# Sample tokens of two heads in one score product, and no products with 32 weight columns

## Chip, cores, metric

One core of a Trainium2 chip runs the whole kernel. The metric is the device time of one execution in microseconds, the median of the runs shown. Its engines are TensorE (PE, with weight loads as PEld), VectorE (DVE), ScalarE (ACT), GpSimd (POOL) and SyncE (SP, which issues most DMAs).

## What is computed

One layer of a streaming encoder for 1,024 prompt tokens and 32 sample tokens. Two branches of it matter here. Branch A is attention with 16 heads of width 64 over 2 key and value heads; a sample token reads 128 cached keys and the 32 new ones:

```python
kblk = jnp.concatenate([k_prev.astype(ka.dtype), ka], axis=1)[:, None]
vblk = jnp.concatenate([v_prev.astype(va.dtype), va], axis=1)[:, None]
...
s = jnp.einsum('bnqkgd,bnskd->bnkgqs', q, k).astype(jnp.float32) * (A_HEAD_DIM ** -0.5)
s = s + bias.astype(jnp.float32)[None, None]
...
m = jnp.maximum(jnp.max(s, axis=-1, keepdims=True), sink)
p = jnp.exp(s - m)
denom = jnp.sum(p, axis=-1, keepdims=True) + jnp.exp(sink - m)
return jnp.einsum('bnkgqs,bnskd->bnqkgd', (p / denom).astype(v.dtype), v)
```

Branch B is a gated linear recurrence with 8 heads and a state of 128 × 128, evaluated in blocks; the 32 sample tokens are a block of their own with a state that is given:

```python
o = jnp.einsum('bhld,bhdv->bhlv', q_ * jnp.exp(b_), state)
a = jnp.einsum('bhtd,bhsd->bhts', q_ * jnp.exp(b_ - b_mid), k_ * jnp.exp(b_mid - b_))
o = o + jnp.einsum('bhts,bhsv->bhtv', jnp.where(causal, a, 0.0), v_)
state = (jnp.exp(b_last)[:, :, 0, :, None] * state
         + jnp.einsum('bhsd,bhsv->bhdv', k_ * jnp.exp(b_last - b_), v_))
```

The outputs of both are gated, projected and added, and a feed-forward part follows. It takes more than half of the time and the change doesn't touch it.

## The kernel before

Tokens stand in three groups, `GR`: 384, 384 and 288 columns; group 2 holds 256 prompt tokens and the 32 sample tokens (from column `SO` = 256). `token_tiles` cuts the groups into nine tiles of 128 tokens, the last of which has the 32 sample tokens. Large products run in float32r, as three products of a high and a low part. Transposes are products of float32 with the identity as the moving operand, so that what is transposed is the weight operand, and a tile of 32 tokens is one of 32 weight columns. The products inside the recurrence are plain float32, and the profile shows each as two passes.

*Attention.* `stream` runs over blocks of gate and query projections, and hands out small steps between half blocks ("half-steps"). Eight pairs of heads `i` follow each other; pair `i`'s nine tiles `j` are spread over the half-steps `lo_` to `hi_` of one pair: `scores(i, j)` at some half-step, `turn(i, j)` three later, `values` five later. Pair 7 has six half-steps for its nine tiles. `q_out` writes the queries of a pair, one head per buffer (`qa`, `qb`), each as high and low part over 128 partitions; for group 2 the columns behind the 288 are zeroed on GpSimd. `scores` makes, per head, two products (parts of the keys, `K1` and `K2`), adds the bias and takes the extremum in one DVE instruction (L457), copies the sink on GpSimd (L455), takes the exponential on ACT (L462), and scales (L464, L466). For the sample (`j` = 8) each product has 160 columns and 32 used rows, one head beside the other in the free dimension of `sc8`, the one buffer that all pairs share. `turn` transposes the probabilities (L478), four times for the sample, and splits them into high and low parts (`ph`, `pl`); `values` multiplies them with `Vs`. `bias_load` loads a pair's bias from DRAM on SP's queue into one of two buffers (L429) and sets two corners on GpSimd.

*Recurrence.* Pieces of the projections of head h (`qf_unit`, then `io_unit`, 11 pieces each) run on PE, and small steps of head h stand behind them at piece numbers counted from `m0` (the head's first piece) and `m1` = `m0` + 22. `factors` makes the decayed keys `ke`, queries `tq` and `qx`, and `d1`. `k_turn` transposes the keys of a group into `kk` (L1186), `v_turn` the values into `vk` (L1115). `tile_in` makes the state's update (L1207) and the products of keys and queries (L1211 for the sample, L1215 for the others), `tile_out` the outputs (L1247 and L1249), `group_out` transposes back (L1270). For the sample, L1211, L1247 and L1249 use 32 weight columns.

The order of each engine is the order of the text as far as the framework's scheduler keeps it; it sets the waits between engines itself. SP and GpSimd work off their queues in order.

Of the kernel before, what the change touches and what calls it, by code (L numbers as in the profile page):

```python
# [10 lines left out]
F32 = mybir.dt.float32  # L11
# [48 lines left out]
def layer_kernel(  # L60
# [17 lines left out]
    def nm(s):  # L78
        n_names[0] += 1
        return f"{s}_{n_names[0]}"  # L80
# [231 lines left out]
    with right("ap") as ap:  # L312
# [89 lines left out]
        def q_out(i):  # L402
            def out(g, b):
                n = GR[g][1]
                qa = ap.tile([P, 384], F32R, tag="qa", name=nm("qa"), bufs=4)
                qb = ap.tile([P, 384], F32R, tag="qb", name=nm("qb"), bufs=4)
                if g == 2:
                    G.memset(qa[:, n:384].bitcast(F32), 0.0)
                    G.memset(qb[:, n:384].bitcast(F32), 0.0)
                S.mul(qa[0:64, :n], b[0:64, :n], -0.125)  # L410
                V.scalar_tensor_tensor(qa[64:128, :n], b[0:64, :n], -0.125, qa[0:64, :n].bitcast(F32),
                                       op0=ALU.mult, op1=ALU.subtract)
                S.mul(qb[64:128, :n], b[64:128, :n], -0.125)
                V.scalar_tensor_tensor(qb[0:64, :n], b[64:128, :n], -0.125,
                                       qb[64:128, :n].bitcast(F32), op0=ALU.mult, op1=ALU.subtract)
                qs[i, g] = (qa, qb)
            return out
# [3 lines left out]
        def bias_load(i):  # L421

            bias = aq.tile([P, 2, 256], F32, tag="bias", name=nm("bias"), bufs=2)
            for h in range(2):

                row = rb_d[2 * i + h]
                src = bass.AP(tensor=row.tensor, offset=row.offset + 127,
                              ap=[[368, 8], [383, 16], [1, 256]])
                dma(bias[:, h, :], src)  # L429
            G.memset(bias[0:64, :, 192:256], BIG)  # L430
            G.memset(bias[64:128, :, 0:64], BIG)
            biases[i] = bias
            yas[i] = aq.tile([P, T], F32, tag="ya", name=nm("ya"), bufs=2)

        def span(j):
# [5 lines left out]
            return P, (j - 1) * P, 256, 0, ((j - 1, 0, P), (j, P, P))  # L441

        def scores(i, j):
            m_, k0, nk, b0, tl = span(j)
            e_ = b0 + nk
# [3 lines left out]
            for h, q in enumerate(qs[i, g]):  # L449
                o = s[:, h * 256 + b0:h * 256 + e_]  # L450
                E.matmul(o, q[:, c:c + P], K1[kv][:, k0:k0 + nk], start=True, stop=False)
                E.matmul(o, q[:, c:c + P], K2[kv][:, k0:k0 + nk], start=False, stop=True)
            sc = sc8 if j == 8 else aq.tile([P, 2, 260], F32, tag="sc", name=nm("sc"), bufs=5)
            st = aq.tile([P, 2, 2], F32, tag="st", name=nm("st"), bufs=4)
# [15 lines left out]
        def turn(i, j):  # L470
            m_, k0, nk, b0, tl = span(j)
            sc = probs[i, j]
# [3 lines left out]
            for a, (_, kc, _) in enumerate(tl):  # L476
                for h in range(2):
                    E.transpose(t[:, (2 * a + h) * P:(2 * a + h + 1) * P], sc[:, h, kc:kc + P],  # L478
                                ident[:])
            n = 2 * len(tl)  # L480
            ph, pl = (x[:].rearrange("p a b -> p (a b)")[:, :n * m_] for x in (ph, pl))
            if m_ == P:
                split(ph, pl, t[:, :n * P])
            else:
                split(*(x.rearrange("p (a b) -> p a b", b=m_) for x in (ph, pl)),
                      t[:].rearrange("p (a b) -> p a b", b=P)[:, :, :m_])
            probs[i, j] = (ph, pl)
# [361 lines left out]
        bias_load(0)  # L849
        sc8 = aq.tile([P, 2, 2 * P], F32, name="sc8")  # L850
        G.memset(sc8[:], 0.0)
        for b, out in zip(banks[1], outs):
            out(1, b)
        blocks, small = [(lambda w=w: w, 2, out) for w, out in zip(ws, outs)], {}
        for i in range(8):
# [131 lines left out]
    with right("bp") as bp:  # L987
# [120 lines left out]
        def v_turn(h, g):  # L1108
# [4 lines left out]
            t = tr_bank()  # L1113
            for i, (c, m_, smp) in enumerate(token_tiles(g)):
                E.transpose(t[:m_, i * P:(i + 1) * P], vt[:, c:c + m_], ident[:])  # L1115
            S.copy(vk[:, 0:f, :], t[:, :f * P].rearrange("p (a b) -> p a b", b=P))
            if g == 2:
                S.copy(vk_s[:32], t[:32, 2 * P:3 * P])

# [9 lines left out]
        def factors(h, g):  # L1129
# [50 lines left out]
        def k_turn(h, g):  # L1180
# [3 lines left out]
            kk = bp.tile([P, 3, P], F32, tag="kk", name=nm("kk"), bufs=2)  # L1184
            for i, (c, m_, smp) in enumerate(token_tiles(g)):
                E.transpose(t[:m_, i * P:(i + 1) * P], ke[:, c:c + m_], ident[:])  # L1186
            f = 3 if g < 2 else 2
            S.copy(kk[:, 0:f, :], t[:, :f * P].rearrange("p (a b) -> p a b", b=P))
            if g == 2:
                S.copy(kk[:32, 2, :], t[:32, 2 * P:3 * P])  # L1190
                G.memset(kk[32:64, 2, :], 0.0)
                G.memset(kk[64:P, 2, :], 0.0)
            d["kk", g] = kk

        def tile_in(h, j):
# [14 lines left out]
            if smp:  # L1210
                E.matmul(s[:32, 0:32], d1[:, c:c + 32], qx[:, 384:416], start=True, stop=True)  # L1211
                V.tensor_tensor(ai[:32, :32], s[:32, 0:32].bitcast(I32), cmask[:32, :32],
# [23 lines left out]
        def tile_out(h, j):  # L1236
# [9 lines left out]
            vk = vk_s if smp else d["vk", g][:, i, :]  # L1246
            E.matmul(b[:m_, 0:P], am[:, :m_], vk[:], start=True, stop=st is None)  # L1247
            if st is not None:
                E.matmul(b[:m_, 0:P], d["tq", g][:, c:c + m_], st[:], start=False, stop=True)  # L1249
            S.copy(vk[:m_], b[:m_, 0:P])  # L1250
# [36 lines left out]
        for h in range(8):  # L1287
# [871 lines left out]
```

## Time and profile before

| | |
|---|---|
| median of 3 runs | 1993.48 us (1993.47 to 1995.96) |
| profiled execution | 1993.55 us |
| its span, first to last instruction | 1991.8 us |
| PE busy | 1974.8 us |
| granted TensorE clock | 0.999 |

A row of the profile names the line, engine and operation, output and inputs by the program's names, the shapes and the count. For a product, `128*32 128x160` means 128 rows and 32 columns of weights, and a moving operand of 128 × 160. Behind the bar stand busy time, the mean of one in ns, and the engine's idle time ahead of them with what ended it. In the timeline, a row has its start, its duration (of all, where several are merged), and in brackets the idle time ahead of it. Matmuls overlap, since each is counted from its start to its modelled end; what one costs is the distance to the next start.

### The profile page before, as it was taken

The numbers are of one execution on the slowest core, as the hardware profiler recorded it, in microseconds if no ns is written. First come the engines' busy times: TensorE is split into PE (matmuls) and PEld (weight loads), VectorE is DVE, ScalarE is ACT, GpSimd is POOL, SyncE is SP. The second block draws the span as 40 slices with busy tenths as digits, with TensorE's granted clock in tenths as the row PEclk, the third lists the DMA queues.
The fourth block names the chain that finished last, engine by engine and source line by source line (L and its number), as shares of the span: only waits on it lengthen the run. The fifth ranks groups of instructions, "written<-read, shape, count | busy, mean of one in ns | idle before, by whom it ended". The sixth has DMA issues, their size and how long they took to land.

```text
span 1991.8 us, 37378 instructions
## 1 busy us (share of the span) xinstructions
PE 1974.8 (99%) x14303; PEld 1954.3 (98%) x14303; DVE 1422.5 (71%) x3130; ACT 962.7 (48%) x2151; POOL 235.4 (12%) x345
## 2 busy tenths in 40 slices
PE   8999999999999999999999999999999999999998
PEld 8999999999999999999999999999999999999998
DVE  6788888688888888553455778787888884655552
ACT  7555566566666666451225663333333344444332
POOL 1211100000000000002001123333333300000000
PEclk9999999999999999999999999999999999999999
DMA  7622311411111111486558572222222245665542
GB/s 256 169 88 89 98 55 63 142 43 58 58 49 46 46 46 54 140 246 208 170 177 281 183 266 85 66 88 74 76 86 76 86 152 192 214 194 168 167 133 78
DMA packets 253640, 247.48 MB, mean 124 GB/s; under 512 B 13893, under 2 KB 221912, under 8 KB 253461
## 3 DMA queue, kind: packets, MB, share of 16 engines
q1 hardware_dynamic: 245141, 218.59, 35.6%
q0 software_dynamic: 8240, 26.44, 3.7%
q8 instruction: 112, 1.84, 0.4%
q14 instruction: 67, 0.55, 0.1%
q10 hardware_dynamic: 80, 0.07, 0.0%
HBM read 177.56 MB, written 65.32 MB: 122 GB/s over the span
## 4 chain that ended last, share of the span: by engine, by line
PE 91%; DVE 4%; ACT 1%; issue 1%; DMA 1%; POOL 0%; SPq 0%; DVEq 0%; POOLq 0%; ACTq 0%
PE mm L200 14%; PE mm L201 14%; PE mm L202 14%; PE st L1882 7%; PE st L1881 7%; PE st L1880 7%; PE Y L1018 2%; PE G L1021 2%; PE G L1020 2%; PE G L1018 2%; PE Y L1021 2%; PE Y L1020 2%; PE tr L478 1%; PE so L1215 1%; PE Z L1021 1%
## 5 line engine op out<-in xcount | busy, mean ns | idle before, releaser
L1880 PE MATMUL st<-op,wt 128*128 128x264 f32 x1232 | 348.6, 283 | 1.9 <-DVE Sp L1893 1.2
L1882 PE MATMUL st<-op,wt 128*128 128x264 f32 x1232 | 349.8, 284 | 0.0
L1881 PE MATMUL st<-op,wt 128*128 128x264 f32 x1232 | 347.6, 282 | 0.0
L184 DVE TENSOR_TENSOR wl<-wr,wh 128x1024 fp32r<-128x1024 f32 x129 | 157.9, 1224 | 121.4 <-ACT wh L181 111.0
L1880 PEld LDWEIGHTS st<-op,wt 128*128 128x128 f32 x1232 | 231.2, 188 | 3.5 <-DVE Sp L1893 1.7
L1881 PEld LDWEIGHTS st<-op,wt 128*128 128x128 f32 x1232 | 231.4, 188 | 0.0
L1882 PEld LDWEIGHTS st<-op,wt 128*128 128x128 f32 x1232 | 230.8, 187 | 0.0
L181 ACT CAST wh<-wr 128x1024 fp32r<-128x1024 f32 x116 | 121.7, 1050 | 198.0 <-PE mm L201 124.8
L200 PE MATMUL mm<-La,wh 128*128 128x384 f32 (+1 forms) x528 | 174.4, 331 | 0.0
L201 PE MATMUL mm<-Lb,wh 128*128 128x384 f32 (+1 forms) x528 | 170.9, 324 | 0.5 <-DVE Lb L717 0.5
L200 PE MATMUL mm<-ac,wh 128*128 128x352 f32 x528 | 170.6, 323 | 0.0
L202 PE MATMUL mm<-La,wl 128*128 128x384 f32 (+1 forms) x528 | 170.4, 323 | 0.2 <-DVE wl L692 0.2
L202 PE MATMUL mm<-ac,wl 128*128 128x352 f32 x528 | 169.6, 321 | 0.0
L201 PE MATMUL mm<-ac,wh 128*128 128x352 f32 x528 | 169.3, 321 | 0.0
L1640 ACT CAST wt<-wu 128x512 fp32r<-128x512 f32 x126 | 77.9, 619 | 186.6 <-POOL ab L1866 88.3
L200 PE MATMUL mm<-Ra,wh 128*128 128x264 f32 x512 | 145.4, 284 | 0.0
L201 PE MATMUL mm<-Rb,wh 128*128 128x264 f32 x512 | 145.0, 283 | 0.0
L202 PE MATMUL mm<-Ra,wl 128*128 128x264 f32 x512 | 145.0, 283 | 0.0
L1641 DVE TENSOR_TENSOR wt<-wu,wt 128x512 fp32r<-128x512 f32 x126 | 103.0, 820 | 38.8 <-ACT wt L1640 38.8
L462 ACT ACTIVATE sc<-sc,st 128x257 f32<-128x257 f32 (+1 forms) x144 | 69.7, 485 | 79.2 <-DVE st L457 79.0
L201 PEld LDWEIGHTS mm<-Lb,wh 128*128 128x128 f32 x528 | 99.4, 188 | 1.6 <-DVE Lb L717 1.4
L202 PEld LDWEIGHTS mm<-La,wl 128*128 128x128 f32 x528 | 99.3, 188 | 0.5 <-DVE wl L692 0.5
(511 smaller groups left out, 5701.5 us busy)
## 6 DMA issues: line engine op xcount, KB each, us to landing
wr<-in_w_down_dram SPq DMA_DIRECT2D x66, 512.0 KB
wu<-in_w_up_dram SPq DMA_DIRECT2D x42, 512.0 KB
wu<-in_w_in_dram SPq DMA_DIRECT2D x32, 512.0 KB
wr<-in_w_in_dram SPq DMA_DIRECT2D x25, 512.0 KB
ac<-act_d SPq DMA_DIRECT2D x66, 176.0 KB
act_d<-Up SPq DMA_DIRECT2D x21, 528.0 KB
wr<-in_w_out_dram SPq DMA_DIRECT2D x16, 512.0 KB
pw_d<-pw POOLq DMA_DIRECT2D x11, 512.0 KB, 5.7
```

What stands on the lines that cost most here:

```text
L181: S.copy(hi[:], raw[:])
L184: V.tensor_tensor(lo[:], raw[:], hi[:].bitcast(F32), op=ALU.subtract)
L200: E.matmul(ps, wh, a, start=first and n == 0, stop=False)
L201: E.matmul(ps, wh, b, start=False, stop=False)
L202: E.matmul(ps, wl, a, start=False, stop=last and n == len(ks) - 1)
L1018: E.matmul(o, wh, x[0][k], start=first and k == 0, stop=False, skip_group_check=True)
L1020: E.matmul(o, wh, x[1][k], start=False, stop=False, skip_group_check=True)
L1021: E.matmul(o, wl, x[0][k], start=False, stop=k == 3, skip_group_check=True)
L1641: V.tensor_tensor(t[:, 1], src, t[:, 0].bitcast(F32), op=ALU.subtract)
L1880: E.matmul(o, wh, xh, start=first and k == 0, stop=False, skip_group_check=True)
L1881: E.matmul(o, wh, xl, start=False, stop=False, skip_group_check=True)
L1882: E.matmul(o, wl, xh, start=False, stop=k == 3, skip_group_check=True)
```

## The change

In attention, the sample tokens of both heads of a pair become one tile of 64 rows. Their queries stand side by side in `qa`, the second head's copied there on GpSimd; one product each for `K1` and `K2` gives both heads' scores; a bias tile of its own (`bias8`, one buffer, loaded on SP in the same way) and sinks of both heads in `nsink8` make one addition, one exponential and one scaling; two transposes follow. In the recurrence, the sample's values are copied on GpSimd into the key tile behind its keys and transposed with them, in `k_turn`, which now comes after `v_turn`; L1211, L1247 and L1249 take 128 weight columns, the added ones zero. The buffers change in size to fit.

```diff
                 if g == 2:
-                    G.memset(qa[:, n:384].bitcast(F32), 0.0)
-                    G.memset(qb[:, n:384].bitcast(F32), 0.0)
+                    G.memset(qa[:, n + 32:384].bitcast(F32), 0.0)
...
+                if g == 2:
+                    G.tensor_copy(qa[:, n:n + 32], qb[:, SO:n].bitcast(F32))
...
+        def bias_load8(i):
+            bias8 = aq.tile([64, 160], F32, tag="bias8", name=nm("bias8"), bufs=1)
+            for h in range(2):
+                row = rb_d[2 * i + h]
+                src = bass.AP(tensor=row.tensor, offset=row.offset + 127,
+                              ap=[[368, 2], [383, 16], [1, 160]])
+                dma(bias8[32 * h:32 * h + 32, :], src)
+            biases[i, 8] = bias8
             yas[i] = aq.tile([P, T], F32, tag="ya", name=nm("ya"), bufs=2)
...
+        def scores8(i):
+            s, q, kv, m_ = s_bank(), qs[i, 2][0], i // 4, 64
+            E.matmul(s[:, 0:160], q[:, SO:SO + P], K1[kv][:, 1024:1184], start=True, stop=False)
+            E.matmul(s[:, 0:160], q[:, SO:SO + P], K2[kv][:, 1024:1184], start=False, stop=True)
+            st = aq.tile([P, 2, 2], F32, tag="st", name=nm("st"), bufs=4)
+            mx, tot = st[:m_, 0, 0:1], st[:m_, 1, 0:1]
+            G.tensor_copy(sc8[:m_, 160:161], nsink8[:m_, i:i + 1])
+            V.tensor_tensor_reduce(out=sc8[:m_, 0:160], in0=s[:m_, 0:160], in1=biases[i, 8][:],
+                                   scale=1.0, scalar=nsink8[:m_, i:i + 1], op0=ALU.add,
+                                   op1=ALU.min, accum_out=mx)
+            S.activation(sc8[:m_, 0:161], sc8[:m_, 0:161], AF.Exp, bias=mx, scale=-1.0,
+                         accum_out=tot)
+            V.reciprocal(tot, tot)
+            V.tensor_scalar(sc8[:m_, 0:160], sc8[:m_, 0:160], tot, None, op0=ALU.mult)
...
+            if j == 8:
+                for a in range(2):
+                    E.transpose(t[:, a * P:(a + 1) * P], sc8[:, a * P:(a + 1) * P], ident[:])
+                split(*(x.rearrange("p (a b) -> p a b", b=64) for x in (ph, pl)),
+                      t[:, 0:2 * P].rearrange("p (a b) -> p a b", b=P)[:, :, :64])
...
+            small.setdefault(lo_ + (4 if i < 7 else 0), []).insert(0, lambda i=i: bias_load8(i))
             if i < 7:
                 small.setdefault(lo_ + 2, []).insert(0, lambda i=i: bias_load(i + 1))
...
-        vk_s, am_s = (bp.tile([P, n], F32, name=nm("z")) for n in (P, 32))
+        vk_s, am_s = (bp.tile([P, P], F32, name=nm("z")) for _ in range(2))
...
             for i, (c, m_, smp) in enumerate(token_tiles(g)):
+                if smp:
+                    d["vt_s"] = vt[:, c:c + m_]
+                    break
                 E.transpose(t[:m_, i * P:(i + 1) * P], vt[:, c:c + m_], ident[:])
...
-            qx = bt("qx", 576, 3)
+            qx = bt(*(("qx", 576, 2) if g < 2 else ("qx2", 416, 1)))
...
+            if g == 2:
+                for t in (d1, d["tq", g]):
+                    G.memset(t[:, n:GMAX], 0.0)
...
+                if smp:
+                    G.tensor_copy(ke[:, c + m_:c + 2 * m_], d.pop("vt_s"))
+                    m_ *= 2
                 E.transpose(t[:m_, i * P:(i + 1) * P], ke[:, c:c + m_], ident[:])
...
                 S.copy(kk[:32, 2, :], t[:32, 2 * P:3 * P])
+                S.copy(vk_s[:32], t[32:64, 2 * P:3 * P])
...
-                E.matmul(s[:32, 0:32], d1[:, c:c + 32], qx[:, 384:416], start=True, stop=True)
+                E.matmul(s[:, 0:32], d1[:, c:c + P], qx[:, 384:416], start=True, stop=True)
...
-            E.matmul(b[:m_, 0:P], am[:, :m_], vk[:], start=True, stop=st is None)
+            E.matmul(b[:, 0:P], am[:], vk[:], start=True, stop=st is None)
             if st is not None:
-                E.matmul(b[:m_, 0:P], d["tq", g][:, c:c + m_], st[:], start=False, stop=True)
+                E.matmul(b[:, 0:P], d["tq", g][:, c:c + P], st[:], start=False, stop=True)
...
-            at(m1 + 6, k_turn, h, 2)
-            at(m1 + 8, v_turn, h, 2)
+            at(m1 + 7, v_turn, h, 2)
+            at(m1 + 8, k_turn, h, 2)
```

More of the change, by code (lines that the diff above doesn't have):

```diff
@@ L441, in span @@
             return P, (j - 1) * P, 256, 0, ((j - 1, 0, P), (j, P, P))
+        def scores8(i):
[12 more added lines that the diff above has]
+            V.tensor_scalar(sc8[:m_, 0:160], sc8[:m_, 0:160], tot, None, op0=ALU.mult)
         def scores(i, j):
+            if j == 8:
+                scores8(i)
+                return
             m_, k0, nk, b0, tl = span(j)
@@ L452, in scores @@
                 E.matmul(o, q[:, c:c + P], K2[kv][:, k0:k0 + nk], start=False, stop=True)
-            sc = sc8 if j == 8 else aq.tile([P, 2, 260], F32, tag="sc", name=nm("sc"), bufs=5)
+            sc = aq.tile([P, 2, 260], F32, tag="sc", name=nm("sc"), bufs=5)
             st = aq.tile([P, 2, 2], F32, tag="st", name=nm("st"), bufs=4)
@@ L471, in turn @@
             m_, k0, nk, b0, tl = span(j)
-            sc = probs[i, j]
+            sc = probs.get((i, j))
             ph = aq.tile([P, 2, 2 * P], F32R, tag="ph", name=nm("ph"), bufs=4)
@@ L475, in turn @@
             t = tr_bank()
[L476 to L483, printed above, removed]
-            else:
-                split(*(x.rearrange("p (a b) -> p a b", b=m_) for x in (ph, pl)),
-                      t[:].rearrange("p (a b) -> p a b", b=P)[:, :, :m_])
+            n = 2 * len(tl) * m_
+            ph, pl = (x[:].rearrange("p a b -> p (a b)")[:, :n] for x in (ph, pl))
+            if j == 8:
+                for a in range(2):
+                    E.transpose(t[:, a * P:(a + 1) * P], sc8[:, a * P:(a + 1) * P], ident[:])
+                split(*(x.rearrange("p (a b) -> p a b", b=64) for x in (ph, pl)),
+                      t[:, 0:2 * P].rearrange("p (a b) -> p a b", b=P)[:, :, :64])
+            else:
+                for a, (_, kc, _) in enumerate(tl):
+                    for h in range(2):
+                        E.transpose(t[:, (2 * a + h) * P:(2 * a + h + 1) * P], sc[:, h, kc:kc + P],
+                                    ident[:])
+                split(ph, pl, t[:, :n])
             probs[i, j] = (ph, pl)
@@ L849, in layer_kernel @@
         bias_load(0)
-        sc8 = aq.tile([P, 2, 2 * P], F32, name="sc8")
+        sc8 = aq.tile([P, 2 * P], F32, name="sc8")
         G.memset(sc8[:], 0.0)
+        nsink8 = aq.tile([64, 8], F32, name="nsink8")
+        for h in range(2):
+            z = slice(32 * h, 32 * h + 32)
+            G.tensor_copy(nsink8[z], nsink[z].rearrange("p (i h) -> p i h", h=2)[:, :, h])
         for b, out in zip(banks[1], outs):
@@ L1114, in v_turn @@
             for i, (c, m_, smp) in enumerate(token_tiles(g)):
+                if smp:
+                    d["vt_s"] = vt[:, c:c + m_]
+                    break
                 E.transpose(t[:m_, i * P:(i + 1) * P], vt[:, c:c + m_], ident[:])
             S.copy(vk[:, 0:f, :], t[:, :f * P].rearrange("p (a b) -> p a b", b=P))
-            if g == 2:
-                S.copy(vk_s[:32], t[:32, 2 * P:3 * P])
         def decay(h):
```

## The prediction

> **What bounds the kernel.** I read the first parts of the page, then busy time by stretch, then the timeline of TensorE around the sample instructions.
>
> ```profile
> PE 1974.8 (99%) x14303; PEld 1954.3 (98%) x14303; DVE 1422.5 (71%) x3130; ACT 962.7 (48%) x2151; POOL 235.4 (12%) x345
> ...
> PE 91%; DVE 4%; ACT 1%; issue 1%; DMA 1%; POOL 0%; SPq 0%; DVEq 0%; POOLq 0%; ACTq 0%
> ```
>
> TensorE (PE) is busy for 99% of the span and carries 91% of the chain that ended last. Busy time of overlapping matmuls says little by itself, so the next view matters more: the two stages that the diff touches, cut into stretches. Columns are the stretch, its length, then busy time of PE, PEld, DVE, ACT and POOL, the granted clock, the DMA share and GB/s.
>
> ```profile
> 92.00:345.00 253.00, 253.00 (x1774) 251.81 (x1774) 210.89 (x656) 144.95 (x442) 26.20 (x103) 1.00 0.24 78
> 345.00:370.00 25.00, 23.98 (x172) 23.28 (x171) 15.94 (x53) 13.36 (x40) 0.93 (x6) 1.00 0.15 53
> ...
> 412.00:842.00 430.00, 428.49 (x2851) 420.12 (x2852) 353.98 (x1003) 267.80 (x721) 3.19 (x16) 1.00 0.20 60
> ```
>
> Through nearly all of attention (92 to 345 us) PE has no idle time at all: 253.00 of 253.00, at full clock. Only pair 7, whose nine score tiles are squeezed into half a unit's steps, has a hole of 1.0 us (345 to 370). In the recurrence (412 to 842) 1.5 us are missing out of 430. So a PE slot saved in these stages should come off the end almost whole, as long as no other engine becomes late. DVE at 211 of 253 us is the nearest to that.
>
> **The change, part by part.** Busy times of PE overlap, so I cost by the distance between starts.
>
> *Scores of the sample tokens.* Before, four products of 160 columns (two heads, K1 and K2) per pair; after, two. Transposes before four, after two.
>
> ```profile
> 140.26 0.24 PE L451 MATMUL s<-K,qa 128*128 128x160 f32 x1
> ...
> 140.67 0.34 PE L200 MATMUL mm<-La,wh 128*128 128x288 f32 x1
> ...
> 446.36 0.49 PE L1115 MATMUL tr<-ident,vt 128*128 128x128 f32 x3
> 446.69 0.39 PE L1247 MATMUL so<-vk,am 128*128 128x128 f32 x2
> ```
>
> The four products (two of L451, two of L452) last from 140.26 to 140.67, 0.41 us; two fewer save half of it, 0.20. Three transposes of the same size in the recurrence last 0.33 us, 0.11 each; two fewer save 0.22. Per pair 0.42 us, over eight pairs 3.4 us.
>
> *The sample product of the recurrence.* Per head, six passes (each f32 product runs as two) have 32 weight columns.
>
> ```profile
> 462.26 0.33 PE L1021 MATMUL X<-La,wt 128*128 128x384 f32 x1
> 462.43 0.38 PE L1247 MATMUL so<-vk,am 128*128 128x128 f32 x2
> 462.65 0.39 PE L1249 MATMUL so<-S,tq 128*128 128x128 f32 x2
> 462.87 0.39 PE L1207 MATMUL so<-z,kk 128*128 128x128 f32 x2
> 463.19 0.25 PE L1211 MATMUL so<-qx,d 128*32 128x32 f32 x2
> 463.37 0.55 PE L1186 MATMUL tr<-ident,ke 128*128 128x128 f32 x3
> ...
> 467.26 0.34 PE L1021 MATMUL Y<-TH,wt 128*128 128x384 f32 x1
> 467.53 0.41 PE L1247 MATMUL so<-z,z 128*32 128x128 f32 x2
> 467.78 0.38 PE L1249 MATMUL so<-S,tq 128*32 128x128 f32 x2
> 468.09 0.55 PE L1270 MATMUL tr<-ident,vk 128*128 128x128 f32 x3
> ```
>
> With 128 weight columns, from the start of the L1021 product to the work behind L1249: 462.87 − 462.26 = 0.61 us. With 32, the same sequence: 468.09 − 467.26 = 0.83. The 0.22 us sit at the seams, 0.27 instead of 0.17 on the way in and 0.31 instead of 0.22 on the way out. At L1211 it costs 0.10 to get in (0.32 after L1207 instead of 0.22), while its two passes and the way out take only 0.18. After, two passes with 128 weight columns and 32 moving columns: no row shows that form; by the passes of L1207 it is at most 2 × 0.11 = 0.22, by L1211 itself at least 0.18 less the seam of 0.10. I take 0.22, as passes with 128 moving columns are 0.11 apart and products with 160 are 0.10 apart: at these widths the distance doesn't follow the moving columns. So L1207 and L1211 go from 0.50 to 0.44: 0.06 saved (0.20 at the lower end).
>
> The Trainium skill, "TensorEngine Tiling (Array Packing)", section Tiling Modes, says that a change of tiling mode drains TensorE; the 0.10 us at each seam between 128 and 32 columns agrees with it.
>
> *Values and keys transposed as one.* One transpose per head goes. The three at 446.36 above are those of group 2, and the third has 32 weight columns: 0.11 each, so the narrow one shows no seam. After, `v_turn` has two and `k_turn` three, the third with 64 weight columns. That form has no row; between its neighbours of 32 and 128 columns I take 0.11, and as the dear end 0.11 + 2 × 0.10, the seams of the narrow products. The saving is one transpose, 0.11.
>
> By the same rule of the Trainium skill ("TensorEngine Tiling (Array Packing)", Tiling Modes) 64 columns are a mode of their own, so the dear end would hold and the whole would be 1.6 us less. Another sentence of the Trainium skill on that page (Restrictions and Gotchas) says that column tiling and the transposing of float32 exclude each other; by that the cheap end holds, and the 0.33 us of the three transposes agree with it.
>
> Per head 0.22 + 0.06 + 0.11 = 0.39 us, over eight heads 3.1 us.
>
> *What is added.* Per pair: a GpSimd copy of the second head's queries beside the first's (for a memset that goes), two small loads of the sample's bias on SP. Per head: two GpSimd memsets and one GpSimd copy of the values beside the keys; `k_turn` of group 2 moves two pieces later (m1 + 6 to m1 + 8), `v_turn` one earlier. DVE loses one bias addition and one scaling per pair, ACT one exponential.
>
> ```profile
> L455 POOL COPY sc<-nsink 128x2 f32<-128x2 f32 x64 | 15.2, 240 | 199.6 <-PE tr L478 79.8 <-DVE st L464 27.9 <-DVE sc L466 24.2
> ```
>
> ```profile
> 423.74 0.45 DVE L1174 TENSOR_TENSOR ke<-ke,tf 128x288 f32<-128x288 f32 x1
> 441.36 0.49 PE L1186 MATMUL tr<-ident,ke 128*128 128x128 f32 x3
> ...
> 146.76 0.46 DVE L414 SCALAR_TENSOR_TENSOR qb<-mm,qb 64x288 fp32r<-64x288 f32 x1
> 147.28 0.19 POOL L455 COPY sc<-nsink 128x2 f32<-128x2 f32 x1
> 149.33 0.34 DVE L457 CUSTOM_DVE_ANT_0 sc<-s,bias,nsink 128x128 f32<-128x128 f32 x1
> ```
>
> A GpSimd copy takes 0.24 us here. In the recurrence GpSimd is busy for 3.19 of 430 us, and the keys of group 2 are finished at 424.2, 17 us before PE turns them, so the copy into them is hidden; without that cover PE would wait out the copy, 0.24 us a head. In attention the query copy must wait for L414 (ends at 147.22), and behind it on GpSimd stands the sink copy of the next score tile, now at 147.28. That goes to about 147.5, while the bias addition of its tile starts only at 149.33, and the exponential that needs both comes after. Cost nothing; margin 1.6 us.
>
> ```profile
> 108.34 1.24 SPq L429 DMA_DIRECT2D bias<-rb_d  x2
> 117.36 0.32 SPq L293 DMA_DIRECT2D ta_d<-gt  x1
> 142.06 0.37 DVE L457 CUSTOM_DVE_ANT_0 sc<-s,bias,nsink 32x160 f32<-32x160 f32 x1
> ```
>
> The new bias tile has one buffer, so its load waits in SP's queue for the sample scores of the pair before. Behind it stand the stores of the gates and the weight loads. The load of the next pair's bias waits there for the same scores now (108.34, 1.24 us for two issues), and the next thing SP has to do comes 9 us later; the tile is wanted 34 us later. Cost nothing; without that cover 1.24 us of SP's time a pair.
>
> The moved `k_turn` takes along its three transposes, three copies on ACT and two memsets on GpSimd. Who waits for it is `tile_in` of tile 6, three pieces later (m1 + 11), where it was five; a piece lasts over 1.6 us (twelve products of 288 or 384 columns), the copies under 1 us. In the last head that tile comes at m1 + 8 and so right behind it, but there it came right behind `v_turn` before, and waited for a like copy:
>
> ```profile
> 828.52 0.49 PE L1115 MATMUL tr<-ident,vt 128*128 128x128 f32 x3
> 829.47 0.49 PE L1207 MATMUL so<-vk,kk 128*128 128x128 f32 x2
> ```
>
> Three transposes (0.33) and two products (0.44) leave under 0.2 us of wait there, before as after.
>
> *What doesn't arrive.* In pair 7 PE waits for DVE before the transposes behind the sample scores:
>
> ```profile
> 354.92 0.63 PE L478 MATMUL tr<-ident,sc 128*128 128x128 f32 x4 [0.71 <-DVE pl L224]
> ```
>
> The 0.20 us that the shorter score product saves just ahead of it make that wait longer, unless DVE's shorter list ends it sooner too; I take off 0.2.
>
> **The sum.** 3.4 + 3.1 − 0.2 = 6.3 us. The starts are given to 0.01 us; 0.04 a pair or head make ±0.3 on it. The profiled execution took 1993.55 us (1.75 us outside the span); the median of the runs shown is 1993.48. Forecast: 1993.55 − 6.3 = 1987.3 us.
>
> **The rivals.**
>
> A. *Attention gains nothing*: DVE or ACT is late at the end of each pair, as in pair 7, and PE waits out what it saved. DVE's 83% from 92 to 345 us speaks for it; against it that PE has no hole there, and that DVE and ACT both lose work. Only 3.1 us are left: 1990.4.
>
> B. *The seams aren't due to the 32 columns* but to a wait:
>
> ```profile
> L1247 PEld LDWEIGHTS so<-z,z 128*32 128x32 f32 x16 | 1.1, 108 | 2.0 <-DVE wt L941 1.7 <-issue 0.2
> ```
>
> This row puts the idle time ahead of the narrow L1247 down to DVE. If so, the way in stays, and L1211 with wider weights only loses. Against it: L1249 leaves the narrow form with the same extra 0.09, where nothing is named. Recurrence then gives 0.11 − 0.04 a head, 0.6 us; with attention's 3.4 it is 4.0: 1989.6.
>
> C. *The 64-column transpose brings a new seam*, 0.20 us a head, 1.6 us: 1988.9. For it speaks that the products of 32 columns have seams; against it, that the 32-column transposes have none. The page of the Trainium skill named above speaks for both.
>
> D. *DVE's relief also fills pair 7's hole* of 1.0 us and the like at the stage ends: 1993.55 − 6.5 − 1.0 = 1986.1 (6.5 without the 0.2 taken off).
>
> E. *Slower: GpSimd gets into the path.* The query copy waits for L414 and holds the sink copy, the exponential, the scaling and so the transposes of the next tile. Once the sink copy is over 1.6 us late, the chain is exposed; its length is a sink copy 0.24, two exponentials and a scaling:
>
> ```profile
> 142.36 0.50 ACT L462 ACTIVATE sc<-sc,st 128x257 f32<-128x257 f32 x1
> 143.19 0.61 DVE L466 TENSOR_SCALAR sc<-sc,st 128x256 f32<-128x256 f32 x2
> ```
>
> 0.24 + 2 × 0.50 + 0.61 = 1.85 us a pair, 14.8 in all against 6.3 gained: 2002. The sink copies' long waits (199.6 us of idle time ahead of 64) show that they come late in general, but they wait for old buffers and PE never waits behind them.
>
> **Numbers.** Chances: forecast 0.64, A 0.13, B 0.07, C 0.06, D 0.05, E 0.05. A difference under 0.2% (4.0 us) can't be told from none here. Faster by more: forecast, C, D and half of B, 0.64 + 0.06 + 0.05 + 0.035, about 0.79. Within: A and half of B, about 0.16. Slower: E, 0.05. The range goes from D (1986.1, less half of the 1.1 us that L1211's lower end would add in eight heads) to A (1990.4, with the 0.3 of rounding): 1985.5 to 1990.7, and leaves out little more than E.
>
> **What would show it.** In the profile after: two L451-like products of 160 columns and two transposes per pair instead of four and four; no form with 32 weight columns but the first stage's; 0.17 and 0.22 at the former seams; the two passes of L1211 0.11 apart; five transposes in group 2 per head. PE at 100% from 92 to about 341. The forecast is wrong if PE shows waits that come back once per pair or per head, for POOL or for DVE, or if a stage end has grown a hole over 1 us.

## The result, and the profile after

The changed kernel takes 1988.44 us in the median of 12 runs (1987.82 to 1990.5), the kernel before 1994.16 in 12 runs beside it (1992.5 to 1995.96): a ratio of 0.9971, interval 0.9963 to 0.9979. That is 5.7 us less, between 4.2 and 7.4. The profiled execution took 1987.85 us, against 1993.55 before; the spans, from the first to the last instruction, are 1985.7 and 1991.8.

The page of the changed kernel, busy time and the chain of waits that ended last:

```profile
PE 1966.3 (99%) x14263; PEld 1950.2 (98%) x14263; DVE 1416.7 (71%) x3106; ACT 961.3 (48%) x2135; POOL 241.1 (12%) x371
...
PE 77%; DVE 3%; ACT 1%; issue 0%; DMA 0%; POOL 0%; DVEq 0%; ACTq 0%; POOLq 0%
```

There are 40 products fewer: 32 in attention (two score products and two transposes a pair), 8 in the recurrence (one transpose a head). TensorE is still busy for 99% of the span. The chain could be followed back only to 363.9 us here, so its shares add up to 81% and can't be set against the 91% of before; of what was followed, TensorE has 77 of 81. The same stretches by engine, moved by what was saved until then (columns as before the change):

```profile
92.00:342.00 250.00, 250.00 (x1750) 249.04 (x1749) 206.96 (x635) 142.27 (x427) 25.98 (x102) 1.00 0.25 80
342.00:367.00 25.00, 23.93 (x172) 23.23 (x171) 15.81 (x50) 13.39 (x39) 1.53 (x9) 1.00 0.14 52
409.00:836.00 427.00, 425.08 (x2842) 421.82 (x2843) 352.98 (x1003) 269.56 (x721) 7.96 (x38) 1.00 0.20 61
```

No hole has opened in attention: 250.00 of 250.00. Pair 7's is 1.07 us where it was 1.02, and in the recurrence 1.92 us are missing where 1.51 were. The starts around the sample scores of pair 1 (TensorE's timeline):

```profile
140.49 0.29 PE L202 MATMUL mm<-La,wl 128*128 128x288 f32 x1
140.62 0.24 PE L455 MATMUL s<-K,qa 128*128 128x160 f32 x1
140.69 0.28 PE L456 MATMUL s<-K,qa 128*128 128x160 f32 x1
140.81 0.33 PE L200 MATMUL mm<-La,wh 128*128 128x288 f32 x1
```

Two products in 0.19 us, from 140.62 to 140.81, where four took 0.41. And TensorE's timeline in head 0 of the recurrence:

```profile
459.27 0.33 PE L1056 MATMUL X<-La,wt 128*128 128x384 f32 x1
459.44 0.38 PE L1290 MATMUL so<-vk,am 128*128 128x128 f32 x2
459.66 0.39 PE L1292 MATMUL so<-S,tq 128*128 128x128 f32 x2
459.88 0.39 PE L1250 MATMUL so<-z,kk 128*128 128x128 f32 x2
460.11 0.31 PE L1254 MATMUL so<-qx,d 128*128 128x32 f32 x2
460.25 0.53 PE L1228 MATMUL tr<-ident,ke 128*128 128x128 f32 x3
460.53 0.38 PE L1053 MATMUL G<-La,wt 128*128 128x288 f32 x1
...
464.14 0.33 PE L1056 MATMUL Y<-TH,wt 128*128 128x384 f32 x1
464.31 0.38 PE L1290 MATMUL so<-z,z 128*128 128x128 f32 x2
464.53 0.39 PE L1292 MATMUL so<-S,tq 128*128 128x128 f32 x2
464.75 0.49 PE L1313 MATMUL tr<-ident,vk 128*128 128x128 f32 x3
465.00 0.43 PE L1053 MATMUL Z<-TH,wt 128*128 128x384 f32 x1
```

From L1056 to L1313 the sample's output products now take 0.61 us like those of a full tile (0.83 before). L1250 to the transposes of the keys takes 0.37 (0.50 before), and the two passes of L1254 are 0.14 of it.

**Where the time went, stage by stage.** A single profile's span can't resolve a part of this change, because the start of the kernel takes a different time in each execution. So I compare distances within a profile, between the starts of four kinds of product: the first sample score product of pair 0, the first of the four sample value products of pair 7, and the transpose of the sample's outputs (`tr<-ident,z`, the last of group 2's three) in heads 0, 6 and 7. All from TensorE's rows, in us; the experiments' profiles, each described below, are in the same table, which the rest refers to.

| profile | start of the first sample scores | attention, from there to pair 7's sample values | to head 0 | heads 1 to 6 | head 7 |
|---|---|---|---|---|---|
| before | 105.31 | 262.56 | 110.92 | 324.72 | 43.47 |
| e8, before again | 108.05 | 262.62 | 110.91 | 324.68 | 43.04 |
| e10, before, bias later | 110.49 | 262.58 | 110.94 | 324.73 | 42.76 |
| after | 106.21 | 258.73 | 110.46 | 322.12 | 43.62 |
| e6, after again | 109.02 | 258.73 | 110.52 | 322.08 | 43.23 |
| e1, attention alone | 105.62 | 258.77 | 110.92 | 324.76 | 43.75 |
| e2, recurrence alone | 106.84 | 262.61 | 110.45 | 322.08 | 43.22 |
| e3, L1290 and L1292 narrow | 108.91 | 258.76 | 110.76 | 323.68 | 43.59 |
| e7, L1254 narrow | 106.74 | 258.75 | 110.64 | 322.84 | 43.62 |
| e4, bias8 later | 106.04 | 258.73 | 110.50 | 322.12 | 43.94 |
| e9, bias8 later again | 105.56 | 258.74 | 110.50 | 322.08 | 43.19 |
| e5, both loads later | 105.12 | 258.73 | 110.50 | 322.08 | 43.85 |
| e12, both later again | 106.09 | 258.75 | 110.53 | 322.08 | 43.32 |
| e11, bias8 twice | 107.86 | 258.88 | 110.49 | 322.08 | 43.26 |

In the first profile attention gains 3.83 us, head 0 gains 0.46, and heads 1 to 6 gain 2.60, 0.43 each. Head 7 loses 0.15 and the part ahead of the first sample scores 0.90. Together that is 5.84 less. Behind head 7 the span is another 0.3 shorter, which doesn't reach the time of the execution: from TensorE's last product to the end of the span it is 4.22 us in place of 4.66, but an execution of the changed kernel spends 2.12 to 2.24 us outside its span (twelve runs), where the profiled one of before spent 1.75. Why either moved isn't shown. The two needn't go together: in e1, e5, e11 and e12 the way to the end is as short (4.06 to 4.24 us), and the time outside is 1.69 to 1.81.

### The profile page after: what moved, and what is told of

Read it like the earlier page. It is cut to its first block, busy times and chain, and to the rows that moved or that the text cites. A ratio compares the mean times of both kernels' runs of the same rounds, so it can differ in the third digit from the quotient of the medians.

```text
span 1985.7 us, 37321 instructions
## 1 busy us (share of the span) xinstructions
PE 1966.3 (99%) x14263; PEld 1950.2 (98%) x14263; DVE 1416.7 (71%) x3106; ACT 961.3 (48%) x2135; POOL 241.1 (12%) x371
## 4 chain that ended last, share of the span: by engine, by line
PE 77%; DVE 3%; ACT 1%; issue 0%; DMA 0%; POOL 0%; DVEq 0%; ACTq 0%; POOLq 0%
PE mm L200 11%; PE mm L201 11%; PE mm L202 11%; PE st L1925 7%; PE st L1924 7%; PE st L1923 7%; PE Y L1053 2%; PE G L1056 2%; PE G L1055 2%; PE Y L1055 2%; PE Y L1056 2%; PE G L1053 2%; PE Z L1053 1%; PE so L1258 1%; PE Z L1055 1%; PE Z L1056 1%
## 5 line engine op out<-in xcount | busy, mean ns | idle before, releaser
L181 ACT CAST wh<-wr 128x1024 fp32r<-128x1024 f32 x116 | 121.7, 1050 | 195.4 <-PE mm L201 144.2
L200 PEld LDWEIGHTS mm<-La,wh 128*128 128x128 f32 x528 | 99.4, 188 | 0.1
```

The lines of the kernel that those rows point to most:

```text
L181: S.copy(hi[:], raw[:])
L200: E.matmul(ps, wh, a, start=first and n == 0, stop=False)
```

## The experiments

**Each part alone.** In e1 the recurrence (the diff from `vk_s, am_s` on) is as before; in e2 it is attention that is as before (the diff up to `bias_load8`'s place in `small`).

> Attention's part of the change alone; the recurrence is as before. Theory: TensorE saves 0.45 us a pair, eight times, and loses 0.9 us in pair 0, where the new bias load stands ahead of the weight loads in SP's queue: the span goes from 1991.8 to about 1989.1 us, and the drift against before grows by 0.45 us from one pair's sample scores to the next. Rival 1 (the loss in pair 0 is a chance of that one profile): 1988.2. Rival A of the prediction (attention gains nothing, the wait moves to DVE): 1991.8 or more.

> The recurrence's part alone; attention is as before. Theory: 0.44 us a head, less 0.5 us in the last head: the span goes from 1991.8 to about 1988.8 us, and nothing changes in attention, with no loss in pair 0. If the last head's 0.5 us came from attention's shift of all later times, it isn't lost here: 1988.3. Rival B of the prediction (the seams aren't due to 32 weight columns): 1991.2.

e1: median 1990.52 us against 1995.03 before, ratio 0.9975 (0.9964 to 0.9986), span 1988.2. e2: 1992.02, ratio 0.9988 (0.9979 to 0.9996), span 1990.3. By its span e1 matches the first rival and e2 falls between theory and rival B. Neither reading holds, as the table shows: e2's first sample scores start 1.53 us late, in a stage that e2 leaves as before. Within the stages the parts are clean: 262.56 − 258.77 = 3.79 us in attention alone with nothing in the recurrence, and 0.47 + 2.64 us in the recurrence alone with nothing in attention. Rival A falls with the first, rival B with the second.

**The columns of the output products.** e3 is the changed kernel with this edit:

```diff
-            E.matmul(b[:, 0:P], am[:], vk[:], start=True, stop=st is None)
+            E.matmul(b[:m_, 0:P], am[:, :m_], vk[:], start=True, stop=st is None)
...
-                E.matmul(b[:, 0:P], d["tq", g][:, c:c + P], st[:], start=False, stop=True)
+                E.matmul(b[:m_, 0:P], d["tq", g][:, c:c + m_], st[:], start=False, stop=True)
```

> The whole change, but the sample's output products (L1290 and L1292) with 32 weight columns as before. Theory: the two seams come back, 0.22 us a head: the span is 1985.7 + 1.8 = 1987.5 us, and the starts around them stand 0.83 us apart in place of 0.61. Rival B (a wait for DVE made the distance, not the columns): within 0.3 us of 1985.7.

Median 1991.82 us, ratio to before 0.9979 (0.997 to 0.9988). Heads 1 to 6 take 323.68 us in place of 322.08 to 322.12: about 0.26 a head is given back, 2.1 us in eight. TensorE's timeline of this kernel at the place shown above:

```profile
466.91 0.34 PE L1056 MATMUL Y<-TH,wt 128*128 128x384 f32 x1
467.18 0.41 PE L1290 MATMUL so<-z,z 128*32 128x128 f32 x2
467.42 0.38 PE L1292 MATMUL so<-S,tq 128*32 128x128 f32 x2
467.73 0.55 PE L1313 MATMUL tr<-ident,vk 128*128 128x128 f32 x3
468.03 0.42 PE L1053 MATMUL Z<-TH,wt 128*128 128x384 f32 x1
```

The seams are back: 0.27 us on the way in and 0.31 on the way out, 0.82 from L1056 to L1313. Since only the number of weight columns differs, it makes them. The three transposes behind are dearer as well, 0.30 us to the next start (0.30 in the kernel before, too), where they take 0.25 in the changed kernel (464.75 to 465.00); with the 0.21 of the seams that is the 0.26.

**The columns of the key and query product.** e7 is the changed kernel with this edit:

```diff
-                E.matmul(s[:, 0:32], d1[:, c:c + P], qx[:, 384:416], start=True, stop=True)
+                E.matmul(s[:32, 0:32], d1[:, c:c + 32], qx[:, 384:416], start=True, stop=True)
```

> The whole change, but the sample's product of keys and queries (L1254) with 32 weight columns as before. The prediction's 0.06 us a head would give a drift against the change as it is of 0.06 us from head to head, 0.5 in all; the starts in the profile of the changed kernel (0.37 us from L1250 to the transposes of the keys against 0.50 before) say 0.13 a head, 1.0 in all. If the columns didn't matter here, no drift.

Heads 1 to 6 take 322.84 us, 0.72 to 0.76 more than changed, 0.12 to 0.13 a head. That is one profile and one run (1989.22 us), but this distance varies by 0.08 at most between profiles of a like recurrence. TensorE's timeline:

```profile
460.49 0.39 PE L1250 MATMUL so<-z,kk 128*128 128x128 f32 x2
460.81 0.25 PE L1254 MATMUL so<-qx,d 128*32 128x32 f32 x2
460.99 0.55 PE L1228 MATMUL tr<-ident,ke 128*128 128x128 f32 x3
461.29 0.38 PE L1053 MATMUL G<-La,wt 128*128 128x288 f32 x1
```

0.50 us from L1250 to L1228, as before the change: 0.32 to get in, 0.18 for the rest.

**Controls.** e6 is the changed kernel, e8 the kernel before, each once more.

> The changed kernel once more, as a control for the start and the last head. Theory (what is lost in pair 0 hangs on when the first weights land): the 0.44 us a head and 0.45 us a pair come back to 0.02 us, while the drift at the sample scores of pair 0 is another one than the +0.90 us of the first profile, and the loss between 76 and 81 us lies between 0 and 2 us. Rival (the losses in pair 0 and in the last head are fixed prices of the change): +0.9 in pair 0 and 0.5 in the last head again.

> The kernel before once more, as a control. Theory: the same distances from pair to pair and from head to head as in its first profile, to 0.02 us; a start that may differ by 1 to 3 us by the time of the first sample scores; no stall at the first values of pair 0, since its weight load is issued 1.3 us earlier than in the changed kernel. If a stall of over 0.3 us shows there too, the position of the bias8 load is not what decides it.

e6: median 1988.93 us against 1995.73 before, ratio 0.9967 (0.9955 to 0.9979). Its attention and its heads 1 to 6 repeat the first profile's to 0.04 us, but the first sample scores start at 109.02 in place of 106.21, and head 7 takes 43.23 in place of 43.62: the loss there isn't a fixed price. e8 (1996.05 us in one run) shows the same of the kernel before: stages as in its first profile to 0.06 us, the first sample scores 2.74 us later, head 7 0.43 shorter.

**The first weight load.** The part ahead of the first sample scores had a loss of 0.90 us in the first profile. SP's queue there, of the kernel before:

```profile
70.07 1.30 SPq L429 DMA_DIRECT2D bias<-rb_d  x2
71.47 0.40 SPq L171 DMA_DIRECT2D wr<-in_w_in_dram  x1
```

and of the changed one, with the two bias8 loads (L441) between:

```profile
70.00 1.30 SPq L430 DMA_DIRECT2D bias<-rb_d  x2
71.35 1.31 SPq L441 DMA_DIRECT2D bias<-rb_d  x2
72.78 0.40 SPq L171 DMA_DIRECT2D wr<-in_w_in_dram  x1
```

The weights are asked for 1.31 us later. ACT must cast them (L181), and in its order the cast of the probabilities that TensorE needs next (`ph`, L223) stands behind. Where ACT waits for the weights, TensorE waits as long for `ph`; the timelines of ACT and TensorE in e3, where it is largest with the change's order on SP:

```profile
79.81 1.04 ACT L181 CAST wh<-wr 128x1024 fp32r<-128x1024 f32 x1 [1.63 <-DMA wr<-in_w_in_dram]
...
81.39 0.39 PE L531 MATMUL o<-ph,Vs 128*128 128x256 f32 x1 [1.63 <-ACT ph L223]
```

In the five profiles with the change's order on SP the two waits are equal to 0.01 us: 0.23 (first profile), 0.95 (e1), 1.63 (e3), 0.16 (e6) and 1.03 (e7). The three without a bias8 load (before, e2, e8) show 0, 0.19 and 0.74 us of ACT's wait, and no wait of TensorE for `ph` at this place; in e8 TensorE waits 0.27 us there for `Vs`, whose cast stands behind that of the weights as well. Two edits move loads behind the weights. e4, and e9 once more, move the first bias8 load:

```diff
-            small.setdefault(lo_ + (4 if i < 7 else 0), []).insert(0, lambda i=i: bias_load8(i))
+            small.setdefault(lo_ + (12 if i == 0 else 4 if i < 7 else 0), []).insert(
+                0, lambda i=i: bias_load8(i))
```

e5, and e12 once more, also move the bias load of pair 1, which e10 does in the kernel before:

```diff
-                small.setdefault(lo_ + 2, []).insert(0, lambda i=i: bias_load(i + 1))
+                small.setdefault(lo_ + (14 if i == 0 else 2), []).insert(
+                    0, lambda i=i: bias_load(i + 1))
```

(In e4, e5, e9 and e12 the buffer `yas[i]` is still taken where it was.) e11 goes the other way and issues the first bias8 loads a second time, into a spare buffer.

> The whole change, but the first pair's two bias8 loads are issued eight half-steps later on SP, behind the first weight loads. Theory: the weights land about 1 us earlier, the stall of TensorE at 78.7 us goes, and the sample scores of pair 0 come 0.5 to 0.9 us earlier than with the change as it is: span 1984.8 to 1985.2 us. Rival (the loss in pair 0 has another cause, such as GpSimd's added work or the traffic of the start): the stall stays, 1985.7.

> The whole change, but in pair 0 both the bias load of pair 1 and the bias8 load of pair 0 stand twelve and eight half-steps later in the text, so that SP issues the first weight load 1.3 us earlier than the kernel before and 2.6 us earlier than the change as it is. Theory (in five profiles so far TensorE's loss at 76 to 80 us is how far the weights land behind a fixed point of its own progress, and this load needed 4.4 to 6.0 us from issue to landing): the weights land before ACT asks for them, ACT's cast of them shows no wait, TensorE has no stall behind ph, and the drift doesn't grow between 76 and 81 us. Against the change as it is 0.6 to 2 us less. Rival (the loss comes from another part of the attention edit): the stall at the first values stays at 0.5 us or more although the weights are there.

> The kernel with the bias8 load alone later, a second time. So far TensorE lost between 70 and 102 us, against the first profile of the kernel before: 0.73, 1.16, 2.17, 0.67 and 1.78 us with the change's order on SP (five profiles, mean 1.3), 0, 0.20 and 0.97 with the order of before (mean 0.4), 1.46 in the first profile with the bias8 load later, where the weights needed 6.0 us from issue to landing. Theory (issue time and landing decide): 0 to 1.0 this time, if the weights need 4.4 to 5.5 us. Rival (the bias8 load's place has nothing to do with it): over 1.0 again at a landing of under 5.5 us.

> The kernel before with the bias load of pair 1 twelve half-steps later, and nothing of the change. Theory (the first weight load stands too late on SP in the kernel before as well, by 1.3 us less than in the changed one): TensorE loses 0 to -0.2 us between 70 and 102 us, where the kernel before lost 0, 0.20 and 0.97; 0.2 to 0.8 us off the median. Rival (the order only matters with the change): no difference.

> The whole change, and in pair 0 the two bias8 loads are issued twice, the second time into a buffer that nobody reads. Theory: the first weight load is issued another 1.3 us later, and TensorE loses as much more between 70 and 102 us: about 2.6 us (1.9 to 3.5) in place of 1.3 in the mean of five profiles. Rival (no matter): 0.7 to 2.2 as before, and near 1.3.

> The version with both loads later, once more, beside the kernel before with its bias load later. Theory: no loss between 70 and 102 us again (-0.3 to 0.2), median 1.2 to 2.1 us below that of the changed kernel, and about 8 us below that of the kernel before. If its first result was chance, it comes out like the changed kernel: ratio 0.9967 to the kernel before.

What TensorE lost between 70 and 102 us (how much later than in the first profile of before the same gate products start at the end of that stretch than at its beginning), and the medians:

| kernel | lost from 70 to 102 us | median, ratio to before |
|---|---|---|
| before; e2; e8 | 0; 0.20; 0.97 | |
| the change's order on SP: after, e1, e3, e6, e7 | 0.73; 1.16; 2.17; 0.67; 1.78 | after 1988.44, 0.9971 (0.9963 to 0.9979) |
| e4; e9 (bias8 later) | 1.46; 0.41 | e4 1988.24, 0.9965 (0.9952 to 0.9979); e9 1986.66 in one run |
| e5; e12 (both later) | −0.18; −0.19 | 1986.84, 0.9958 (0.9946 to 0.9971); 1988.42, 0.9968 (0.9956 to 0.9981) |
| e10 (before, bias later) | 3.53 | 1995.67, 1.0003 (0.9994 to 1.0012) |
| e11 (bias8 twice) | 0.61 | 1988.55 in one run |

The theory that the place of the bias8 load decides the loss held only in part. With both loads later the loss is gone twice; but these two kernels also lack a second wait, at L391 between 86 and 92 us (for a cached key or an exponential), which takes 0.30 to 0.97 us in the other twelve profiles, 0.50 in the first of before. In e4 the weights are issued early, at 70.75 us, and are cast at 76.79; TensorE then waits 0.94 us for `Vs`. In e9, the same kernel, ACT doesn't wait for them. And e10 issues its weights early too, at 71.17 us, and loses the most; its timelines:

```profile
77.67 1.04 ACT L181 CAST wh<-wr 128x1024 fp32r<-128x1024 f32 x1 [1.93 <-DMA wr<-in_w_in_dram]
...
79.04 0.39 PE L501 MATMUL o<-ph,Vs 128*128 128x256 f32 x1 [1.68 <-ACT ph L223]
```

And e11, with the weights issued at 75.90, loses less than any of the five. Its timeline of ACT says why:

```profile
79.19 0.56 ACT L223 CAST ph<-tr 128x512 fp32r<-128x512 f32 x1
...
80.55 1.05 ACT L181 CAST wh<-wr 128x1024 fp32r<-128x1024 f32 x1 [0.79 <-DMA wr<-in_w_in_dram]
```

Here the scheduler put `ph` ahead of the weights: ACT waits 0.79 us for them, and TensorE shows no wait for `ph` at all. So the wait reaches TensorE through the order of ACT's queue, and what decides its size is that order and the landing. From issue to the cast it took 4.2 (e12) to 6.5 us (e10) in the profiles where ACT waited, a spread larger than the 1.3 us that the bias8 load costs. Each edit near the first pair also reorders ACT there, so how much of the loss the bias8 load itself makes stays open: the means of the five and the three profiles are 1.30 and 0.39 us, an estimate of 0.9 with such a scatter. For the same reason no better version is shown: e5's interval lies mostly below that of the change, e12's hardly differs from it, and 0.4 us of e5's lead lies outside the span.

**The last head.** Its distance varies from 42.76 to 43.94 us, mostly for one wait. TensorE's rows of it, of e8 (the kernel before):

```profile
815.69 0.49 PE L1247 MATMUL so<-vk,am 128*128 128x128 f32 x2 [0.61 <-DVE S L1225]
```

of the changed kernel:

```profile
807.75 0.49 PE L1290 MATMUL so<-vk,am 128*128 128x128 f32 x2 [1.37 <-DVE S L1268]
```

and of e4:

```profile
807.92 0.49 PE L1292 MATMUL so<-vk,am 128*128 128x128 f32 x2 [1.67 <-DVE S L1270]
```

TensorE waits for the state, which DVE makes after it has split a weight tile that ACT cast late. Of ACT's waits between 796 and 850 us, those for weight DMAs come to 3.8 us in e8 and 4.5 in the changed kernel; in all 14 profiles they are 3.07 to 3.17 us longer than TensorE's wait, so the two go together. With the recurrence as before head 7 takes 43.26 us in the mean of four profiles, in the ten profiles of a changed one 43.48. Without that wait it takes 42.41 to 42.43 us with the recurrence as before, and 42.26 to 42.30 in the eight profiles with the whole of its part (e7 42.41, e3 42.59). So besides the wait the head gains 0.14 us, not 0.43, and the wait, 0.35 to 1.67 us long, is longer by 0.34 in the mean of these eight.

Most of the missing 0.29 lies at one place. TensorE's rows ahead of a later output product of head 7, in the kernel before:

```profile
822.52 0.49 PE L1186 MATMUL tr<-ident,ke 128*128 128x128 f32 x3
822.85 0.39 PE L1247 MATMUL so<-vk,am 128*128 128x128 f32 x2
823.07 0.39 PE L1249 MATMUL so<-S,tq 128*128 128x128 f32 x2
```

and in the changed one, where `k_turn` comes later and its three transposes no longer stand there:

```profile
816.75 0.34 PE L202 MATMUL X<-La,wl 128*128 128x384 f32 x1
817.08 0.49 PE L1290 MATMUL so<-vk,am 128*128 128x128 f32 x2
817.41 0.39 PE L1292 MATMUL so<-S,tq 128*128 128x128 f32 x2
```

The product ahead takes 0.33 us to the next start, where the same product takes 0.17 to 0.18 in the kernel before, and L1290 takes 0.33 where L1247 took 0.22: together 0.26. DVE finishes the state at 822.65 and 817.03 us. Before, TensorE was still at the transposes then; in all ten profiles with the new order this product starts 0.05 to 0.06 us behind the end of the state, so I take it for a wait, though the view names none there and no run moves `k_turn` alone.

## Why the prediction was right, step by step

The forecast was 1987.3 us, range 1985.5 to 1990.7, against 1988.44 measured. Against the kernel before in the same runs the time fell by 5.7 us, where 6.3 were forecast; by the spans it fell by 6.1. That the total came so near is in part luck. In the first profile attention gained 3.8 us where 3.2 were forecast (3.4 less the 0.2 of pair 7), and the recurrence 2.9 where 3.1 were; the start took 0.9 back and the time outside the span 0.4, and neither of these was in the sum.

*Scores and transposes of a pair.* 0.20 us was forecast for the scores; it is 0.22 (0.41 to 0.19). With the transposes 3.4 us were forecast for eight pairs, and 3.8 arrived in every profile with this part (3.7 in e11). The mechanism held; the term was a tenth too small: scores and transposes give 0.22 and 0.23 a pair, 3.6 in all, and the other 0.2, in the projections' products around them, is not explained. *Pair 7*: the 0.2 taken off was wrong in size. The row that carries it,

```profile
352.40 0.63 PE L514 MATMUL tr<-ident,sc 128*128 128x128 f32 x4 [0.77 <-DVE pl L224]
```

shows a wait of 0.77 us in place of 0.71 (0.77 to 0.78 in all ten profiles with this part, 0.70 to 0.71 in the four without): DVE's shorter list brought the wait's end forward by most of what the scores saved, as that paragraph had left possible. Rival D would have needed the hole to close; it is 1.07 us.

*The sample's output products.* 0.22 us a head forecast, 0.21 between the same two starts; the 0.05 of the transposes behind weren't counted. That 32 weight columns make the seams is shown by e3. The rule of the Trainium skill, "TensorEngine Tiling (Array Packing)", Tiling Modes, that a change of mode drains TensorE agrees with the 0.10 and 0.09 us at the two seams of e3.

*L1211, now L1254.* A step that failed by size: "I take 0.22", for two passes with 128 weight and 32 moving columns. They take 0.14, so the product saves 0.13 a head and not 0.06 (e7: 0.12 to 0.13). The reason given, that at these widths the distance doesn't follow the moving columns, doesn't hold down to 32 of them; the lower end in the text, 0.20 saved, was too far the other way.

*The merged transpose.* The cheap end held: the three transposes of L1228, the last of 64 columns, take 0.28 us to the next start (460.25 to 460.53), where those of L1186, the last of 32 columns, took 0.30 before; in e7, with the product ahead as before, they take 0.30 as well. The two left in `v_turn` take 0.22 in place of 0.33. There is no seam, so rival C falls, and with it the reading of the Trainium skill, "TensorEngine Tiling (Array Packing)", Tiling Modes, by which 64 columns are a mode of their own here. The sentence of the Trainium skill on the same page, Restrictions and Gotchas, that column tiling and the transposing of float32 exclude each other fits. The parts don't add up exactly: 0.26 + 0.13 + 0.11 is 0.50, and a head gains 0.44. Counted by distances between starts in heads 1 to 6, the products of the projections take about 0.1 us a head more in the changed kernel, by a hundredth in each of many places; why isn't known.

*The last head* was forecast to gain like the others; it gained nothing, and that is the step of the sum that failed outright. Two things were left out of it: the wait for the state, which lasts as long as the weights take, and the moved `k_turn`. The prediction asked who waits for that one and found cover; but its transposes themselves had covered a second wait for the state, and by the rows above about 0.26 us of it came into the open. So the recurrence's 3.1 us came out near (2.9 in the first profile) with a larger size for seven heads, 0.40 to 0.47 for head 0 and 2.6 for the next six, and none for the eighth.

*What is added.* GpSimd's copies lie where they were expected; their groups by line:

```profile
L416 POOL CAST qa<-qb 128x32 fp32r<-128x32 f32 x8 | 1.8, 224 | 6.4 <-DVE qb L413 6.4
...
L483 POOL COPY sc<-nsink 128x2 f32<-128x2 f32 x64 | 15.1, 240 | 192.8 <-PE tr L514 108.6 <-ACT sc L490 19.8 <-DVE qa L410 14.8
...
L1226 POOL COPY ke<-vt 128x32 f32<-128x32 f32 x8 | 2.7, 338 | 110.3 <-DVE d L1180 68.3 <-PE tr L1228 42.1
```

No instruction waits for L1226, and no row of TensorE's in attention names GpSimd: rival E had no part. L1226 takes 0.34 us in the mean, not the 0.24 of the sink copies, at no cost under that cover.

*The bias loads on SP*: "Cost nothing; without that cover 1.24 us of SP's time a pair." For pairs 1 to 7 that held: no loss repeats from pair to pair. For pair 0 the cover wasn't there. I had read SP's queue around 108 us, where the load of pair 2's bias stands, and not at 70 us, where the same text is issued during the start with the first weights right behind it. The price of one such pair in SP's time was in the sentence (1.24 us; it took 1.31), and nothing was put into the sum for it. What it costs TensorE stays open, as said above: an estimate of 0.9 us with a scatter as large.

## What to carry to other kernels

Where TensorE has no idle time over a stage, the distance between starts, taken from rows of that stage, gives what an instruction costs there to a few hundredths of a microsecond; the last head, where it waits for something else, gave almost nothing back. When a step is moved, ask not only who waits for it, but also which wait it had covered where it stood. A load that is put into a queue once per loop pass has a first pass in which that queue is in another state: look at that one by itself, and at what stands behind the waiting instruction on the next engine. When executions differ by 3 us in their first 100 us, compare distances between like instructions within a profile, not spans.

## What the runs showed of the hardware

Narrow weights cost mostly in their seams, and only for some products: two neighbours of 32 and 128 weight columns cost 0.09 to 0.10 us more at each change (e3), and 0.05 in the transposes behind, while a transpose with 64 weight columns behind two of 128 cost none (0.28 to 0.30 us for the three to the next start, 0.30 with 32 columns). Two passes with 128 weight and 32 moving columns took 0.14 us, where two with 128 moving columns took 0.22 to 0.23 in the rows beside them. And the start isn't repeatable as the rest is: over 14 profiles the first sample scores came between 105.12 and 110.49 us, while attention behind them, in kernels with the same attention, repeated to 0.06 us (e11 apart).
